# Branch a's gates by seven half-size products a pair, token differences made by transfers in DRAM, and part of a convolution on ScalarE

## The chip, the core and the metric

The kernel runs on one core of a Trainium2 chip. The metric is the device time of one execution in microseconds (us). The core has five engines, each with its own queue of instructions in program order: TensorE (PE; matmuls, with the weight loads shown apart as PEld), VectorE (DVE), ScalarE (ACT), GpSimd (POOL) and SyncE (SP, which issues most transfers). Transfers issued by SP, ACT and POOL run on 16 DMA engines.

## The reference

Two layers of an encoder trunk on 512 tokens of width 1024. Cut to what the change touches:

```python
h = rmsnorm(x, norm_mix[i])
qa, ka, va, glu_in, qc, kc, vc, gates = split(h @ w_in[i])
ya = diff_attention(qa, ka, va, ...)          # 512 wide
yb = conformer_conv(glu_in, ...)              # depthwise, 31 taps, 512 channels, + layernorm
yc = neighbourhood_attention(qc, kc, vc, ...) # 512 wide
ga, gb, gc = split(sigmoid(gates))            # 1024 wide each
merged = ga * (ya @ w_br_a[i]) + gb * (yb @ w_br_b[i]) + gc * (yc @ w_br_c[i])
x = x + merged @ w_o[i]
# then a SwiGLU FFN and a gated per-layer embedding
```

## The kernel before

Everything is kept transposed: 128 channels on the partitions, 512 tokens along the row. A product with a 1024 x 128 block of weights is a loop over 8 chunks of 128 input channels. To keep float32 accuracy in the PE's rounded format (fp32r), every operand is a sum of a high and a low half, and each chunk takes three matmuls (`mm3`, L176 to L181: high x high, high x low, low x high). The halves come from `split` (L162): ACT copies the source into the high half (L143) and DVE subtracts it for the low half (L157).

`weights` (L168) loads a block by SP into `wr` and splits it into `wh` and `wl`, three buffers of each tag. It runs at a raised priority, so that the scheduler places it early. `gemm` (L183) makes a block's products and calls `chunk()` after each chunk. Every four chunks are a tick, on which delayed work (attention units, norms) is emitted into PE's order. PE's order is the order of emission; the other engines' rows are ordered by a list scheduler at build time, by priority and by its own estimate of when inputs are ready, and then run strictly in that order.

A layer (`layer`, L434) runs: GLU inputs; neighbourhood attention (`natten`, branch c); differential attention (`diff`, branch a); gates c (`gate_c`, L751, eight blocks); gates b 0 and 1; branch c (`branch_c`, L758: eight products, each multiplied into `acc[m]`); gates b 2 and 3; `merge_a` (L765); gates b 4 to 7, with parts of the per-layer input between them; `merge_b` (L783); the output product; the FFN; the per-layer embedding.

`merge_a` takes, for each of eight output blocks, a gate product (8 chunks, 24 matmuls of 512 columns), a sigmoid on ACT, a branch product (4 chunks, 12 matmuls), a multiplication and an addition into `acc[m]` on DVE.

The depthwise convolution is DVE's background work. `taps` (L541) is a generator of 4 x 31 operations, each a multiply-add over 128x512 (L160, `conv_z`). `background(after, n)` (L556) emits the next n of them behind a given instruction; the table `BG` says how many at which place. Whatever is left is emitted at the head of `conv` (L568), which sums the four blocks (`conv_ss`), splits the sum (`conv_rp`), and has PE form the mean over channels two ticks later (L581), then the variance and the result for `merge_b`.

The FFN already uses products of half the size. For a pair of blocks (gate g, up u) and a pair of chunks, `seven` (L964) makes both 2 x 2 products of half-size quarters with seven products instead of eight: sums of weights s1 to s4 and differences of activations t1 to t4. Two of the sums are made by accumulating transfers (`accum_op`, L979), which POOL issues. `sevens_of` (L1096) interleaves the pieces of one pair with those of the next.

Each row's right factor `rb` (the rms factor) comes at the start of a layer; `scaled` (L244) multiplies the eight chunks of x by it and makes the high and low halves `h`.

Of the kernel before, what the change touches and what calls it, by code (L numbers as in the profile page):

```python
# [30 lines left out]
CON3W = 31  # L31
HALO = CON3W // 2
NA_KR = 8
NA_KC = 16
# [19 lines left out]
GAP = 144  # L54
BACC = dict(dynamic_dma_scratch_size=1024)
# [6 lines left out]
class Net:  # L62
# [181 lines left out]
    def scaled(self, xs):  # L244

        for k, x in enumerate(xs):
            yield 1
            self.tt(x, x, self.rb, ALU.mult)
            self.hs.append(self.operand(x, self.par(self.i, "mix", k), "h"))

    def main_norm(self, sq, waits=(2, 2), x=None):
# [46 lines left out]
    def build(self):  # L298
        nc, tc, a = self.nc, self.tc, self.a
        self.bufs = dict(wr=3, wh=3, wl=3, h=8, qk=2, kh=2, v=4, pt=2, y=5, z=5, x=4, t=7, rp=4,  # L300
                         e=4, a=3, r=2, rb=1, ss=1, sm=8, rc=4, b=2, s=8)
        self.bg, self.w_ahead = BG, 400
        self.pbufs = dict(mm=3, sc=2, tr=2, av=1)
        with tc.tile_pool(name="sb", bufs=1) as self.pool, \
                tc.tile_pool(name="ps", bufs=1, space=PSUM) as self.psum, \
                tc.tile_pool(name="dr", bufs=1, space=DRAM) as dram:
            xs = dram.tile([KD, P, 512], F32, name="xs")
            self.pis = dram.tile([KD, P, 512], F32, name="pis")
            with tc.manual_schedule(engines={mybir.EngineType.PE}):
# [74 lines left out]
    def small(self):  # L384
# [5 lines left out]
        for tag, n in (("b", 2 * NW), ("s", 10), ("sm", 8), ("rc", 4)):  # L390
            self.sb(tag, [P, n])
        for tag, n in (("lam", 2 * L), ("nlam", L), ("subg", L), ("power", 4)):
            self.sb(tag, [P, n], bufs=1)
# [7 lines left out]
    def consts(self):  # L401
# [5 lines left out]
        self.power = self.sb("power", [P, 4], bufs=1)  # L407
        nc.vector.memset(self.power, -0.5)
        self.ones = self.sb("ones", [P, P], bufs=1)
        nc.vector.memset(self.ones, 1.0)  # L410
# [23 lines left out]
    def layer(self, i, h, xsrc, xs):  # L434
        self.i, self.h = i, h
        zs, cs = [], []
        self.todo = self.taps(zs, cs)
        self.glu(zs)
# [22 lines left out]
        for m in range(1, KD):  # L461
            self.gate_c(acc, m)
        for m in range(2):
            self.gate_b(gb, m, AF.Copy, None)
# [3 lines left out]
        for m in range(2, 4):  # L468
            self.gate_b(gb, m, AF.Sigmoid, "sigmoid")
        self.merge_a(ya, acc)  # L470
        conv = self.run(self.conv(cs, yb))
# [69 lines left out]
    def taps(self, zs, cs):  # L541

        for j, z in enumerate(zs):
            zf = z.rearrange("p a b -> p (a b)")
            c = self.sb("z", [P, 512])
            cs.append(c)
            for d in range(CON3W):
                w = self.par(self.i, "cw", j * CON3W + d)
                src = zf[:, d * GR:d * GR + 512]
                if d == 0:  # L550
                    yield self.nc.vector.tensor_scalar(c, src, w, self.par(self.i, "cb", j),
                                                       ALU.mult, ALU.add)
                else:
                    yield self.stt(c, src, w, c, ALU.mult, ALU.add)

    def background(self, after, n):  # L556
# [194 lines left out]
    def gate_c(self, acc, m):  # L751
        self.phase = "gatec"
        ps = self.proj(OFF_G + 2 * D + m * P)
        if m % 2 == 0:
            acc += self.parts_of("x", [512], 2)
        self.background(self.act(acc[m], ps, AF.Copy), self.bg["gatec"])

    def branch_c(self, acc, ys):  # L758
        self.phase = "branchc"
        for m in range(KD):  # L760
# [4 lines left out]
    def merge_a(self, ys, acc):  # L765
        self.phase = "mergea"
        for m in range(KD):
            ps = self.proj(OFF_G + m * P)
            g = self.sb("t", [P, 512])
            self.background(self.act(g, ps, AF.Sigmoid, table="sigmoid"), self.bg["mergea"])  # L770
            pb = self.ps("mm")
            self.gemm(pb, self.a["w_br_a"][self.i, m], ys)
            self.tt(g, g, pb, ALU.mult)
            self.background(self.tt(acc[m], acc[m], g, ALU.add), self.bg["mergea2"])

    def gate_b(self, gs, m, func, table):
        self.phase = "gateb"
        ps = self.proj(OFF_G + D + m * P)
        if m % 2 == 0:
            gs += self.parts_of("v", [512], 2)  # L780
        self.background(self.act(gs[m], ps, func, table=table), self.bg["gateb"])

# [618 lines left out]
def _halves(w):  # L1401

    b = _blocks(w).reshape(L, NFB, P, KD, P)
    return np.ascontiguousarray(b[:, :, :, ORDER]).reshape(L, NFB, P, D)

# [66 lines left out]
def _layout(v):  # L1472
# [4 lines left out]
    for i in range(L):  # L1477
# [15 lines left out]
        "w_0": w_0,  # L1493
        "w_in": _blocks(w_in),
        "w_va": _vblocks(w_in[:, :, OFF_VA:OFF_VA + 512]),
        "w_vc": _wide(w_in[:, :, OFF_VC:OFF_VC + 512]),
# [25 lines left out]
```

## Time and profile before

| what | value |
|---|---|
| median of 3 runs | 1755.6 us (1755.54 to 1755.67) |
| the profiled execution, its own time | 1756.09 us |
| its span in the profile | 1754.3 us, 25072 instructions |
| granted TensorE clock | 0.999 |
| 38 to 71 us (layer 0, natten's values): DVE busy, ACT busy, DMA share | 32.36, 15.54, 0.60 |
| 71 to 127 us (natten): the same | 39.10, 38.43, 0.67 |
| 279 to 329 us (gates b 0 to 3, branch c): the same | 45.59, 23.71, 0.29 |
| 395 to 423 us (gates b 4 to 7): the same | 22.47, 17.13, 0.41 |

A row of the windows view gives a stretch, its length and each engine's busy time in it. A row of the group view gives source line, engine, operation, output <- inputs with their shapes, the count, and behind the bars the busy time, the mean of one in ns, and the idle time before them with what ended it. The end of a matmul is modelled, so the pace of PE is read from the distance between starts. "Landing" is the time from the issue of a transfer to its completion signal.

### The profile page before, as it was taken

The page shows a single profiled execution, that of the slowest core. Times are in us where ns is not written, and L with a number is a line of the kernel's source. Part 1 is how long each engine was busy: PE and PEld are TensorE (multiplying, and loading weights), DVE is VectorE, ACT ScalarE, POOL GpSimd, SP SyncE. Part 2 cuts the span into 40 slices and gives each one's busy share as a digit, 9 for nine tenths or more (in the row PEclk, how much of TensorE's full clock was granted, in tenths as well). Part 3 has the DMA queues.
Part 4 walks back from the last instruction along what each step waited for, and adds up shares of the span by engine and source line. Part 5 has one row for each costly group of instructions (what it writes and reads, how often), then busy time and mean ns, then how long its engine had stood idle before and what let it go on. Part 6 is the DMA issues. An engine that isn't in the chain of part 4 may idle for free.

```text
span 1754.3 us, 25072 instructions
## 1 busy us (share of the span) xinstructions
PE 1747.3 (100%) x8970; PEld 1490.2 (85%) x8970; DVE 1421.7 (81%) x2346; ACT 964.4 (55%) x1729; POOL 104.0 (6%) x114
## 2 busy tenths in 40 slices
PE   9999999999999999999999999999999999999998
PEld 7888888888888888888888898888888988888887
DVE  7967987998799687797776688889887985977876
ACT  5566545226577275574545665553365763745654
POOL 0000000000121020100000000000001210101000
PEclk9999999999999999999999999999999999999999
DMA  6575641334767365543446655323256764755332
GB/s 230 159 192 158 162 126 46 112 100 140 230 162 186 118 171 155 142 119 131 156 130 164 194 150 153 111 73 96 93 176 199 183 172 121 179 143 157 96 105 97
DMA packets 114781, 253.82 MB, mean 145 GB/s; under 512 B 16864, under 2 KB 23776, under 8 KB 114656
## 3 DMA queue, kind: packets, MB, share of 16 engines
q1 hardware_dynamic: 101264, 227.83, 42.3%
q0 software_dynamic: 12672, 23.07, 8.1%
q8 instruction: 71, 1.16, 0.3%
q10 hardware_dynamic: 720, 1.31, 0.2%
q14 instruction: 54, 0.44, 0.1%
HBM read 215.46 MB, written 7.34 MB: 127 GB/s over the span
## 4 chain that ended last, share of the span: by engine, by line
PE 97%; DVE 1%; DMA 1%; ACT 1%; SPq 0%; issue 0%; POOL 0%; POOLq 0%; ACTq 0%; DVEq 0%
PE ffn_mm L1013 6%; PE ffn_sc L1013 6%; PE ffn_mm L180 4%; PE ffn_mm L179 4%; PE ffn_mm L181 4%; PE ffn_mm L1016 3%; PE ffn_sc L1016 3%; PE mergea_mm L180 2%; PE mergea_mm L181 2%; PE mergea_mm L179 2%; PE ffn_tr L1013 2%; PE natten_mm L179 2%; PE natten_mm L180 2%; PE gateb_mm L180 2%; PE gateb_mm L181 2%; PE gateb_mm L179 2%
## 5 line engine op out<-in xcount | busy, mean ns | idle before, releaser
L160 DVE SCALAR_TENSOR_TENSOR conv_z<-glu_z,pre_par,conv_z 128x512 f32<-128x512 f32 x240 | 179.6, 748 | 3.4
L143 ACT ACTIVATE ffn_wh<-ffn_wr 128x1024 fp32r<-128x1024 f32 (+1 forms) x92 | 92.7, 1021 | 99.5 <-PE ffn_mm L180 63.4
L157 DVE TENSOR_TENSOR ffn_wl<-ffn_wr,ffn_wh 128x1024 fp32r<-128x1024 f32 (+1 forms) x92 | 107.1, 1175 | 20.8 <-ACT ffn_wh L143 20.4
L979 POOL DMA_DIRECT2D ffn_qk<-w_fu x88 | 78.0, 992 | 589.3 <-DMA ffn_qk<-w_fu 323.7
L143 ACT ACTIVATE mergea_wh<-mergea_wr 128x1024 fp32r<-128x1024 f32 (+1 forms) x32 | 27.1, 846 | 96.8 <-PE mergea_mm L180 79.6
L157 DVE TENSOR_TENSOR ffn_t<-ffn_mm,wo_rb 128x512 f32<-128x512 f32 (+1 forms) x46 | 31.1, 677 | 51.6 <-PE ffn_mm L181 51.6
L157 DVE TENSOR_TENSOR ffn_wl<-ffn_qk,ffn_wh 128x1024 fp32r<-128x1024 f32 x44 | 53.7, 1220 | 11.0 <-ACT ffn_wh L143 10.9
L143 ACT ACTIVATE diff_a<-diff_sc,diff_s 128x512 f32<-128x512 f32 x32 | 22.0, 688 | 71.6 <-DVE diff_s L893 71.6
L143 ACT ACTIVATE ffn_wh<-ffn_qk 128x1024 fp32r<-128x1024 f32 x44 | 46.7, 1061 | 26.8 <-PE ffn_mm L180 16.2
L179 PE MATMUL ffn_mm<-ffn_v,ffn_wh 128*128 128x512 f32 x132 | 51.4, 389 | 0.0
L180 PE MATMUL ffn_mm<-ffn_v,ffn_wh 128*128 128x512 f32 x132 | 51.4, 389 | 0.0
L181 PE MATMUL ffn_mm<-ffn_v,ffn_wl 128*128 128x512 f32 x132 | 51.3, 389 | 0.0
L179 PE MATMUL ffn_mm<-ffn_y,ffn_wh 128*128 128x512 f32 x132 | 51.3, 389 | 0.0
L180 PE MATMUL ffn_mm<-ffn_y,ffn_wh 128*128 128x512 f32 x132 | 51.3, 389 | 0.0
L181 PE MATMUL ffn_mm<-ffn_y,ffn_wl 128*128 128x512 f32 x132 | 51.3, 389 | 0.0
L143 ACT ACTIVATE natten_wh<-natten_wr 128x1024 fp32r<-128x1024 f32 x24 | 25.4, 1058 | 42.2 <-issue 15.5
L1013 PE MATMUL ffn_sc<-wo_h,ffn_wh 128*128 128x512 f32 x176 | 48.0, 394 | 0.0
L157 DVE TENSOR_TENSOR ffn_t<-ffn_t,ffn_e 128x256 f32<-128x256 f32 x84 | 46.3, 551 | 1.0 <-ACT ffn_e L143 0.9
L893 DVE TENSOR_REDUCE diff_s<-diff_sc 128x1 f32<-128x512 f32 x64 | 42.1, 683 | 2.2 <-PE diff_sc L800 2.2
L1013 PE MATMUL ffn_mm<-wo_h,ffn_wh 128*128 128x512 f32 x160 | 43.6, 394 | 0.0
L225 POOL TENSOR_TENSOR diff_rc<-diff_sm,pre_power 128x4 f32<-128x4 f32 x8 | 8.9, 1115 | 561.8 <-DVE diff_sm L160 503.2
L143 ACT ACTIVATE natten_b<-natten_b,natten_s 128x256 f32<-128x256 f32 x64 | 30.4, 499 | 20.4 <-DVE natten_s L719 20.3
(894 smaller groups left out, 6050.1 us busy)
## 6 DMA issues: line engine op xcount, KB each, us to landing
ffn_qk<-w_fu POOLq DMA_DIRECT2D x88, 256.0 KB, 6.6
ffn_wr<-w_fg SPq DMA_DIRECT2D x44, 512.0 KB, 4.4
ffn_wr<-w_fd SPq DMA_DIRECT2D x32, 448.0 KB, 3.8
ffn_r<-w_fu SPq DMA_DIRECT2D x44, 256.0 KB, 3.1
ffn_qk<-w_fg SPq DMA_DIRECT2D x44, 256.0 KB, 3.3
ffn_qk<-w_fu SPq DMA_DIRECT2D x44, 256.0 KB, 3.4
natten_wr<-w_in SPq DMA_DIRECT2D x16, 512.0 KB, 4.2
diff_wr<-w_in SPq DMA_DIRECT2D x16, 512.0 KB, 4.3
```

The lines of the kernel that those rows point to most:

```text
L143: i = self.nc.scalar.activation(out, in_, func, **kw)
L157: return self.nc.vector.tensor_tensor(out, a, b, op)
L160: return self.nc.vector.scalar_tensor_tensor(out, a, s, b, op0, op1)
L179: mm(out, wh, ah, start=first, stop=False, **kw)
L180: mm(out, wh, al, start=False, stop=False, **kw)
L181: mm(out, wl, ah, start=False, stop=last, **kw)
L225: nc.gpsimd.tensor_tensor(col, ms, self.power, ALU.pow)
L893: nc.vector.tensor_reduce(out=m[:, u:u + 1], in_=sc, op=ALU.max, axis=AX.X, negate=True)
L979: nc.gpsimd.dma_start(q, wu[:, lo], accum_op=ALU.add)
L1013: mm(out, wh[:, c], bs[k][b], start=first and k == 0, stop=False, skip_group_check=True)
L1016: mm(out[:, 0], wl[:, c], bs[k][b][:, 0], start=False, stop=k == 3, skip_group_check=True)
```

## The change

It has three parts.

**Gates of branch a.** `merge_a` now works on four pairs of gate blocks. `gates` makes the two blocks (call them g and u) of a pair by seven products, each of 4 chunks x 3 matmuls of 256 columns, on quarters of the tokens and channels: a11, s1, s3, a12, s2, a22 and s4 are the names of the weights in this text. a11 and a12 lie in g, a22 in u. s1|s2 is the raw tile: SP loads parts of g and u, and two accumulating transfers on POOL (L869 of the changed kernel) add the other part of u. ACT and DVE split it; then DVE overwrites the same tile with the values of s3 and s4, which are split too. There is one raw tile for all pairs. The three accumulators C, A and Q lie in PSUM; ACT copies C into A after a11, A into Q after s3, and A to SBUF after s2, before s4 adds into A. Between a pair's pieces run the two branch products of the pair before (a "fill": 12 matmuls of 512 columns each); beside the first pair they are the last two of branch c, which `branch_c` no longer does. The addition into `acc` is an accumulating transfer on POOL (L943). The gate weights have a rearranged copy `w_ga`.

**Differences of the activations.** `scaled` lets ACT write signed quarter copies of the normalized x to DRAM, where eight transfers on POOL (four plain, four accumulating, L265) form t1 to t4. `differences` loads them beside branch c, and ACT and DVE split them.

**Convolution.** Of the fourth block's 31 taps the first 16 go to ACT (`aside`): number 0 straight into a tile `half`, numbers 1 to 15 each into the one buffer `rb` (`conv_rb`), from where an accumulating transfer on POOL (L593) adds it into `half`. Ten are placed behind gates c, gates b and pairs (`beside`); the last six are emitted at once, when DVE's taps reach the fourth block, and have no such tie. DVE's remaining 15 taps of that block start from `half`. The counts in `BG` are changed so that they sum to the 108 taps left to DVE.

```diff
-BG = dict(glu=2, natten=1, values=3, diff=1, gatec=2, branchc=2, gateb=4, mergea=4, mergea2=2)
+BG = dict(glu=2, natten=2, values=3, diff=1, gatec=2, branchc=1, gateb=4, mergea=2, mergea2=1, mergea3=2)
...
     def scaled(self, xs):
...
+            f, n = self.sb("t", [P, 2, 256]), self.i * KD + k
+            for half in range(2):
+                g = self.par(self.i, "mix", k) if half == k % 2 else self.neg[:, n:n + 1]
+                self.act(f[:, half], x[:, half * 256:half * 256 + 256], AF.Copy, scale=g)
+            self.nc.gpsimd.dma_start(self.fd[:, k % 2 * 2:k % 2 * 2 + 2, k // 2], f)
...
+        for out, src, add in ((t1, b11, 0), (t3, b22, 0), (t1, b12, 1), (t3, b12, 1), (t2, t1, 0),
+                              (t2, b22, 1), (t4, t2, 0), (t4, b21, 1)):
+            yield 4
+            kw = dict(accum_op=ALU.add) if add else {}
+            self.nc.gpsimd.dma_start(out, src, **kw)
...
+                if j == 3 and d == ASIDE:
+                    for _ in self.other:
+                        pass
+                    yield self.stt(c, src, w, self.half, ALU.mult, ALU.add)
...
+    def aside(self, zs):
+        zf = zs[3].rearrange("p a b -> p (a b)")
+        c, t = self.half, self.sb("rb", [P, 512])
+        for d in range(ASIDE):
...
+            if d == 0:
+                yield self.act(c, src, AF.Identity, scale=w, bias=self.par(self.i, "cb", 3))
+            else:
+                i = self.act(t, src, AF.Copy, scale=w)
+                self.nc.gpsimd.dma_start(c, t, accum_op=ALU.add)
+                yield i
...
+    def gates(self, m, out):
...
+            nc.sync.dma_start(raw[:, lo], wg[:, lo])
+            nc.sync.dma_start(raw[:, up], wu[:, up])
+            nc.sync.dma_start(g, wg)
+            nc.sync.dma_start(a22, wu[:, up])
+            for q in (lo, up):
+                nc.gpsimd.dma_start(raw[:, q], wu[:, lo], accum_op=ALU.add)
+            halve(*wide(), g, ("a11", "a12"))
+            halve(self.sb("kh", [P, 512], F32R), self.sb("a", [P, 512], F32R), a22, ("a22",))
+            halve(*wide(), raw, ("s1", "s2"))
+            self.stt(raw[:, lo], raw[:, lo], -1.0, a22, ALU.mult, ALU.subtract)
+            self.tt(raw[:, up], g[:, up], raw[:, lo], ALU.subtract)
+            for name, q, tag in (("s3", lo, "rp"), ("s4", up, "b")):
+                halve(*(self.sb(tag, [P, 512], F32R) for _ in range(2)), raw[:, q], (name,))
+        C, A, Q = (self.ps("mm", (P, 256)) for _ in range(3))
...
+        product(C, "a11", "b11", True)
+        self.act(A, C, AF.Copy)
+        yield
+        T = self.ps("tr", (P, 256))
+        product(T, "s1", "t3", True)
+        self.act(uu[:, 0], T, AF.Copy)
+        product(A, "s3", "t2")
+        self.background(self.act(Q, A, AF.Copy), self.bg["mergea"])
+        product(C, "a12", "b21")
+        self.act(gg[:, 0], C, AF.Sigmoid, table="sigmoid")
+        yield
+        product(A, "s2", "t1")
+        self.act(uu[:, 1], A, AF.Copy)
+        product(Q, "a22", "t4")
+        self.tt(uu[:, 1], uu[:, 1], uu[:, 0], ALU.add)
+        last = self.tt(uu[:, 0], Q, uu[:, 0], ALU.add)
+        product(A, "s4", "b22")
...
+        def gated(a, pb, m):
+            g = gs[m]
+            self.background(self.tt(g, g, pb, ALU.mult), self.bg["mergea3"])
+            self.nc.gpsimd.dma_start(a, g, accum_op=ALU.add)
...
+            for g in (pair, fill, fill, pair, fill, pair):
+                next(g, None)
```

How the rows stand on the engines. ScalarE before, two blocks in the middle of merge_a (`mergea_wh` is a high half of gate or branch weights, `mergea_t` the sigmoid of a gate):

```order
L143 ACTIVATE mergea_wh_3633<-mergea_wr_3632 128x1024
L143 ACTIVATE mergea_wh_3670<-mergea_wr_3669 128x512
L143 ACTIVATE mergea_t_3602<-mergea_mm_3571 128x512
L143 ACTIVATE mergea_wh_3693<-mergea_wr_3692 128x1024
L143 ACTIVATE mergea_wh_3730<-mergea_wr_3729 128x512
L143 ACTIVATE mergea_t_3662<-mergea_mm_3631 128x512
```

ScalarE in the change, pair 2 (the third) from its copy of A into Q on. `mergea_mm_3830` and `_3831` are its C and A, `gatec_v_3026` is the raw tile, `mergea_wh_4002` the high half of the next pair's s1|s2, `mergea_wh_4035` that of the next fill's weights, `mergea_rp` that of s3, and `mergea_t_3834<-mergea_mm_3831` is the copy of A to SBUF after s2:

```order
L144 ACTIVATE mergea_mm_3832<-mergea_mm_3831 128x256
L144 ACTIVATE mergea_wh_3994<-mergea_wr_3986 128x1024
L144 ACTIVATE conv_rb_2806<-glu_z_920,pre_par_69 128x512
L144 ACTIVATE mergea_t_3833<-mergea_mm_3830 128x256
L144 ACTIVATE mergea_wh_4002<-gatec_v_3026 128x1024
L144 ACTIVATE mergea_wh_4035<-mergea_wr_4034 128x1024
L144 ACTIVATE conv_rb_2806<-glu_z_920,pre_par_69 128x512
L144 ACTIVATE mergea_rp_4008<-gatec_v_3026 128x512
L144 ACTIVATE mergea_t_3834<-mergea_mm_3831 128x256
```

Where a sigmoid stood right behind the splits, two taps (`conv_rb`) and three splits now stand ahead of the copy of A; each tap writes the buffer that the transfer of the tap before it reads.

GpSimd had no row between the last norm of branch a and the norm of the convolution (`conv_rc`). In the change, from the first pair's accumulates (`gatec_v`) to the fourth's:

```order
L593 DMA conv_z_374<-conv_rb_2806 128x512
L869 DMA gatec_v_3026<-w_ga 128x512 x2
L943 DMA gatec_x_1975<-mergea_t_3487 128x512
L943 DMA gatec_x_1975<-mergea_t_3488 128x512
L869 DMA gatec_v_3026<-w_ga 128x512
L593 DMA conv_z_374<-conv_rb_2806 128x512
L869 DMA gatec_v_3026<-w_ga 128x512
L943 DMA gatec_x_2652<-mergea_t_3658 128x512
```

Taps (L593), accumulates for the raw tile (L869) and additions into `acc` (L943) share one queue, and a row waits there until its inputs are ready.

VectorE at the end of merge_a, before (`conv_z` taps, `conv_ss` the sum over blocks, `conv_rp` its low half):

```order
L160 SCALAR_TENSOR_TENSOR conv_z_3544<-glu_z_871,pre_par_67,conv_z_3544 128x512 x3
L157 TENSOR_TENSOR pin_wl_3941<-pin_wr_3939,pin_wh_3940 128x256
L160 SCALAR_TENSOR_TENSOR conv_z_3544<-glu_z_871,pre_par_67,conv_z_3544 128x512
L157 TENSOR_TENSOR conv_ss_3867<-conv_ss_3867,conv_z_3544 128x512
L157 TENSOR_TENSOR mergea_t_3842<-mergea_t_3842,mergea_mm_3846 128x512
L157 TENSOR_TENSOR pin_wl_3957<-pin_wr_3955,pin_wh_3956 128x256
L157 TENSOR_TENSOR gatec_x_2884<-gatec_x_2884,mergea_t_3842 128x512
L157 TENSOR_TENSOR conv_rp_3872<-conv_ss_3867,conv_rp_3871 128x512
```

And in the change, from the last pair's quarter add after the copy of A (`mergea_t_4020`), `conv_z_374` being `half`:

```order
L158 TENSOR_TENSOR mergea_t_4020<-mergea_t_4020 128x256
L161 SCALAR_TENSOR_TENSOR conv_z_3900<-glu_z_920,pre_par_69,conv_z_374 128x512
L158 TENSOR_TENSOR mergea_t_4020<-mergea_mm_4018,mergea_t_4020 128x256
L161 SCALAR_TENSOR_TENSOR conv_z_3900<-glu_z_920,pre_par_69,conv_z_3900 128x512
L158 TENSOR_TENSOR pin_e_4211<-pin_t_4208,pin_e_4210 128x512
L161 SCALAR_TENSOR_TENSOR conv_z_3900<-glu_z_920,pre_par_69,conv_z_3900 128x512
L158 TENSOR_TENSOR pin_e_4217<-pin_t_4214,pin_e_4216 128x512
L161 SCALAR_TENSOR_TENSOR conv_z_3900<-glu_z_920,pre_par_69,conv_z_3900 128x512
L158 TENSOR_TENSOR mergea_t_4019<-mergea_t_4019,mergea_sc_4166 128x512
L161 SCALAR_TENSOR_TENSOR conv_z_3900<-glu_z_920,pre_par_69,conv_z_3900 128x512 x3
```

All 15 taps of the fourth block now stand behind the last pair's copy of A, where one of the last few stood before.

More of the change, by code (lines that the diff above doesn't have):

```diff
@@ L462, in layer @@
             self.gate_c(acc, m)
+        self.bs, self.raw = [], self.sb("v", [P, 1024])
         for m in range(2):
@@ L763, in branch_c @@
             self.background(self.tt(acc[m], acc[m], ps, ALU.mult), self.bg["branchc"])
-    def merge_a(self, ys, acc):
-        self.phase = "mergea"
[L767 to L774, printed above, removed]
+            next(quarters, None)
```

134 lines of the change are left out of this document (122 added, 12 removed).

## The prediction

> **What bounds the kernel now.** I read the busy shares first, then the chain that ended last, then PE's waits, then the stretch that the change rewrites.
>
> ```profile
> PE 1747.3 (100%) x8970; PEld 1490.2 (85%) x8970; DVE 1421.7 (81%) x2346; ACT 964.4 (55%) x1729; POOL 104.0 (6%) x114
> PE 97%; DVE 1%; DMA 1%; ACT 1%; SPq 0%; issue 0%; POOL 0%; POOLq 0%; ACTq 0%; DVEq 0%
> ...
> PE pre_av L331 <- DVE pre_zeror L404: 1.1, 1, 1.1
> PE diff_sc L800 <- ACT diff_e L143: 0.2, 1, 0.2
> ...
> 329.00:362.00 33.00, 33.00 (x147) 27.35 (x146) 29.44 (x41) 9.56 (x14) 0.00 (x0) 1.00 0.27 85
> 362.00:395.00 33.00, 33.00 (x148) 27.31 (x147) 29.85 (x41) 8.87 (x14) 0.00 (x0) 1.00 0.33 103
> ```
>
> PE is the chain (97%) and waits 1.3 us in all: a matmul less is time less, and any new wait of PE is time more, at full price. The window rows are merge_a of layer 0 (stretch, length, then busy PE, weight loads, DVE, ACT, POOL, granted clock 1.00, DMA share 0.27 and 0.33). DVE is busy 59.3 of 66 us there, ACT only 18.4. So ACT has room in sum; whether it has it at the right moment is the question.
>
> **What PE saves.** First and last row of a run of 512-wide and of a run of 256-wide matmuls:
>
> ```profile
> 345.30 0.39 PE L179 MATMUL mergea_mm<-glu_h,mergea_wh 128*128 128x512 f32 x1
> ...
> 350.74 0.39 PE L179 MATMUL mergea_mm<-diff_y,mergea_wh 128*128 128x512 f32 x1
> ...
> 495.62 0.28 PE L1020 MATMUL ffn_tr<-wo_v,ffn_wh 128*128 128x256 f32 x1
> ...
> 498.36 0.28 PE L1022 MATMUL ffn_mm<-wo_z,ffn_pt 128*128 128x256 f32 x1
> ```
>
> 24 matmuls of 512 in 5.44 us are 227 ns each; 23 of 256 in 2.74 us are 119 ns. Two gate blocks cost 48 x 0.227 = 10.88 us, seven products 84 x 0.119 = 10.00 us. Saved: 0.88 us a pair, 7.0 us over eight pairs. Nothing else on PE changes. By the Trainium skill ("TensorE: Matmul & The Clock Gate", Back-to-back issue gap) an isolated matmul takes N/2.4 + 2.5 ns, so about 216 and 109 ns, an estimate of 1.2 us a pair and 9.5 us in all; the rows say 227 and 119 with the clock at 1.00, so the sum keeps 7.0.
>
> **Prices of the operations.** These rows price what ACT, DVE and the transfers do in the new merge_a:
>
> ```profile
> L143 ACT ACTIVATE mergea_wh<-mergea_wr 128x1024 fp32r<-128x1024 f32 x7 | 7.4, 1062 | 13.9 <-PE mergea_mm L180 9.6 <-PE gateb_mm L180 4.3
> L143 ACT ACTIVATE mergea_wh<-mergea_wr 128x512 fp32r<-128x512 f32 x7 | 4.4, 633 | 30.2 <-PE mergea_mm L180 30.2
> L143 ACT ACTIVATE gateb_v<-gateb_mm 128x512 f32<-128x512 f32 x4 | 2.3, 579 | 0.0
> L143 ACT ACTIVATE ffn_t<-ffn_mm 128x256 f32<-128x256 f32 x82 | 30.3, 372 | 12.0 <-PE ffn_mm L1016 12.0
> ...
> L160 DVE SCALAR_TENSOR_TENSOR conv_z<-glu_z,pre_par,conv_z 128x512 f32<-128x512 f32 x47 | 35.2, 749 | 0.8
> L157 DVE TENSOR_TENSOR mergea_wl<-mergea_wr,mergea_wh 128x1024 fp32r<-128x1024 f32 x7 | 8.6, 1226 | 1.2 <-ACT mergea_wh L143 0.6
> L157 DVE TENSOR_TENSOR mergea_t<-mergea_t,mergea_mm 128x512 f32<-128x512 f32 x8 | 5.5, 688 | 2.0 <-PE mergea_mm L181 2.0
> L157 DVE TENSOR_TENSOR pin_wl<-pin_wr,pin_wh 128x256 fp32r<-128x256 f32 x1 | 0.4, 426 | 0.1
> ...
> DMA to landing us min/median/max: 4.0/6.6/9.8
> ...
> DMA to landing us min/median/max: 4.4/4.7/5.1
> ...
> L979 POOL DMA_DIRECT2D ffn_qk<-w_fu x88: 862/886/1248, 448.0 to 1621.0; - x88
> mergea_wr<-w_br_a SPq DMA_DIRECT2D x16, 256.0 KB, 2.6
> ```
>
> The only accumulating transfers of before are the FFN's 88 (256 KB each, the size of every new one): 0.9 us on POOL, and 4.0 us at least from issue to landing, 6.6 in the median; the two at 489 to 492 us, where few others run, took 4.4 and 5.1. The change's are SBUF to SBUF, which no row shows, in a stretch with a DMA share of about 0.3. Bounds: 2.6 us (a plain 256 KB load in this very stretch) and 6.6. I take 4.0, the nearest row at the lightest load.
>
> In sum DVE fits. Per pair it has 3 wide low halves (3.7 us), 5 operations of 0.69 to 0.75 for a22, s3 and s4 (3.6), two quarter adds (0.9), two products (1.4) and 7 taps (5.2): 14.8 us beside 15.45 us of PE. The 16 quarter copies in `scaled` (16 x 0.37 = 6 us a layer) and the 16 transfers for the differences I cost at nothing: they have from about 45 to 290 us. Without that cover, NATTEN's weights and stacked transfers would wait; I allow 0 to 4 us a layer.
>
> **What PE loses.** ACT, DVE and POOL run their rows in order (ACT's waits on PE in the rows above show it), so an ACT row that waits for a transfer holds the copies behind it. With a pair's start as 0, PE's pieces end at: a11 1.4, fill 4.2, s1 5.6, s3 7.0, a12 8.4, fill 11.2, s2 12.6, a22 14.0, s4 15.4. s4 adds into A, so it needs ACT's copy of A after s2: only a22 (1.4 us) covers it. Four places follow, per layer:
>
> 1. Front of pair 0. After the last gate_b matmul ACT does an eviction 0.6, a tap 0.6, the split of s1|s2 1.0 and only then that of the fill's weights 1.0; DVE follows with two low halves. The third matmul of the fill finds its low half at 4.7 and should run at 1.9: 2.8 us. The accumulate for s1|s2 stands on POOL behind the tap that waits for gate_b 2 and lands 0.4 us after ACT could use it: 3.2 us.
> 2. End of pairs 0 and 1. Ahead of the copy of A on ACT stand the next pair's s1|s2 split, which itself waits for s2 (its buffer), and the split of the next fill's weights. The copy ends at 12.7 + 1.0 + 1.0 + 0.4 = 15.1 and was due at 14.0: 1.1 us. In pair 0 the raw tile comes free late (low half of s4 at 9.0; plain loads 3.1, then 0.9 + 0.1 on POOL and 4.0 to land: 17.1; copy done 19.5 against 17.2): 2.3 us there.
> 3. End of pairs 2 and 3. The last six taps (10 to 15) share one buffer, so each ACT row waits for the transfer before it: 0.6 + 0.1 + 4.0 us a turn. In pair 2, as worked below, the copy of A ends at 17.8: 3.8 us. In pair 3 the same turns put taps 12 to 15 at 2.4, 7.1, 11.9 and 16.6; then three splits (gate_b's weights, two for pin) and the copy of A at 18.8: 4.8 us.
>
> ```
> POOL  accumulate for pair 3 at 6.5, tap 9 at 7.4, landed 11.4
> ACT   tap 10 11.5-12.1, sigmoid 12.5, s1|s2 of pair 3 (after s2) 12.8-13.8, fill weights 14.7
> ACT   tap 11 (tap 10 landed 12.2+4.0) 16.3-16.9, s3 split 17.4, copy of A 17.8
> ```
>
> 4. The convolution's mean. DVE's 15 taps of the fourth block start from `half`, so after tap 15 has landed, at 20.7 from pair 3's start; PE ends s4 at 20.2. From there DVE does 15 taps (11.2), four operations of 0.69, one of 1.23, two of 0.43 and the last sum (0.69): 16.8, about 15.8 with the overlap of 0.08 that the rows below show between starts and ends. conv_ss is done 0.5 + 15.8 = 16.3 after s4, the split's high half at 17.1. PE wants it after two fills (5.4) and a gate block (5.4), at 10.9: 6.2 us.
>
> ```profile
> 372.65 0.69 DVE L157 TENSOR_TENSOR gatec_x<-gatec_x,mergea_t 128x512 f32<-128x512 f32 x1
> 373.26 2.32 DVE L160 SCALAR_TENSOR_TENSOR conv_z<-glu_z,pre_par,conv_z 128x512 f32<-128x512 f32 x3
> ...
> 396.07 0.69 DVE L157 TENSOR_TENSOR conv_rp<-conv_ss,conv_rp 128x512 fp32r<-128x512 f32 x1
> ...
> 399.70 0.39 PE L581 MATMUL conv_tr<-conv_rp,pre_onesr 128*128 128x512 f32 x1
> ```
>
> Before, the low half was there at 396.8 and PE used it at 399.7: 2.9 us in hand, now gone.
>
> Sum per layer: 3.2 + 2.3 + 1.1 + 3.8 + 4.8 + 6.2 = 21.4; both layers 42.8. The profiled execution took 1756.1 (its span is 1754.3, 1.8 lie around it), 0.5 above the median of 1755.6. So 1756.1 - 7.0 + 42.8 = 1791.9, and 1791 from the median.
>
> **Rivals.**
>
> *The saving alone* (faster): 1755.6 - 7.0 = 1748.6. For it: the FFN runs the same seven products, accumulates and copies with PE at 100% (chain). Against: there, another pair's products lie between s2 and s4, and no tap stands among ACT's copies. 0.10. Some stalls that just eat the saving (within 0.2%): 0.04.
>
> *Only the order costs* (slower): transfers land in 2.6 us, as the plain load does. Then no tap holds ACT: 2.8 + 1.0 + 1.1 + 2.3 (pair 2: the two wide splits, a tap, and s3's split wait for DVE) + 0.9 + 5.2 = 13.3 a layer, 1755.6 - 7.0 + 26.6 = 1775. The Trainium skill ("DMA: Bandwidth & Descriptors", Anatomy of one DMA — SWDGE (gpsimd) path) has 2.0 us fixed plus bytes over 436 GB/s, an estimate of 2.6 us for 256 KB, with most of the fixed part in the receipt, heaviest for HBM. The rows above, all of them into SBUF, never fall below 4.0, so the trace differs so far. 0.27.
>
> *Long transfers* (slower): 6.6 us, the median. Each turn of a tap grows by 2.6: by the same steps 10.9, 2.9, 8.9, 15.1 and 8.7, 46.5 a layer, 1842. It decides where merge_a's transfers collide as the FFN's do; its DMA share of 0.3 speaks against. 0.10.
>
> *A change that does not do what it says*: the order shows all of it done; not weighed further.
>
> **How the numbers follow.** Forecast 0.49 at 1791, order alone 0.27, long 0.10, saving alone 0.10, cancelled 0.04. A measurement of this kernel tells 0.2% (3.5 us) from no change. Faster 0.10, same 0.04, slower 0.86. The range runs from 1766, under the order's 1775 (its small terms may halve), to 1826, part of the way to the long transfers (and the 4 us a layer of early transfers): about 0.2 is left out.
>
> **What would show it.** PE waits on ACT before the s4 products, growing from pair 0 to pair 3, some 4 us in the last two; ACT's `conv_rb` rows waiting on the accumulating transfer; conv's first matmul waiting about 6 us on DVE or ACT; mean pace of 256-wide matmuls 119 ns. The forecast is wrong if those waits are absent, if taps land in under 3 us, or if PE waits in NATTEN.

## The result and the profile after

The changed kernel takes 1828.5 us (median of 4 runs, 1827.6 to 1829.7) against 1755.6 before: ratio 1.0415, 95% interval 1.0397 to 1.0433. It is slower, by 72.9 us; the prediction had +35 and a range that ended at 1826. The profiled execution spans 1827.0 us, so 1828.8 with the 1.8 around it, 72.7 more than the 1756.1 that the prediction started from.

From the page of the changed kernel, busy time by engine and a row of the 40 slices (granted clock in tenths); then PE's waits (engine, line, what it waited for: us in total, times, longest):

```profile
PE 1769.6 (97%) x9258; PEld 1518.3 (83%) x9258; DVE 1427.7 (78%) x2366; ACT 1030.3 (56%) x1867; POOL 182.4 (10%) x208
PEclk9999999898999999999999999998899999999999
```
```profile
PE mergea_mm L180 <- ACT mergea_t L144: 26.5, 8, 5.4
PE branchc_sc L180 <- ACT branchc_wh L144: 8.8, 2, 4.5
PE conv_tr L629 <- ACT conv_rp L144: 8.8, 2, 4.4
PE natten_mm L732 <- DVE natten_t L161: 4.1, 1, 4.1
PE diff_tr L230 <- POOL diff_rc L226: 1.9, 2, 1.4
PE pre_av L349 <- DVE pre_zeror L422: 1.1, 1, 1.1
PE branchc_sc L182 <- DVE branchc_wl L158: 0.6, 2, 0.4
```

Where there was 1.3 us of waiting, there are now 51.8. The first three rows and the last are the places that the prediction named: the s4 products, the first fill, the mean of the convolution, 44.7 us in both layers (42.8 predicted). NATTEN's 4.1 was costed at nothing. And the PE busy time **grew** by 22 us although PE has 7 us less to do: it ran slow. These windows of the changed kernel (stretch, length, busy PE, granted clock, DMA share, GB/s) follow pairs 0 and 1 of layer 0:

```profile
331.00:337.00 6.00, 1.93 (x15) 1.00 0.75 125
337.00:341.00 4.00, 3.38 (x8) 0.57 0.31 90
341.00:352.00 11.00, 11.00 (x78) 1.00 0.70 181
352.00:356.00 4.00, 0.67 (x4) 0.81 0.03 5
356.00:362.00 6.00, 6.00 (x29) 0.56 0.70 235
362.00:374.00 12.00, 11.91 (x81) 1.00 0.70 132
374.00:376.00 2.00, 1.31 (x11) 1.00 0.50 89
376.00:390.00 14.00, 14.00 (x98) 1.00 0.80 198
```

Behind the waits of 4.3 and 3.3 us the granted clock is half for some 3 to 6 us; behind the wait of 0.8 at 374 it is not. Added up over windows of 1 us (busy PE times one minus the clock), 25.6 us go to it in the whole run, 2.9 of them in NATTEN. The Trainium skill ("TensorE: Matmul & The Clock Gate", Part 1: The HAM clock gate) has this rule: after an idle window of about 3.4 us PE drops to half rate until it has been busy for about as long, the window running free. The trace agrees in kind, with a wait of 2.28 us at 1258.4 in layer 1 that was also followed by it.

This table has the time from the first matmul of one stage to the first of the next, read from the rows of PE in the timeline (us); "f2" is the last experiment:

| stretch | before | after | f2 |
|---|---|---|---|
| NATTEN, layer 0 (layer 1) | 88.6 (88.4) | 95.5 (88.4) | 89.7 (88.5) |
| gate_b to merge_a, layers 0, 1 | 49.8, 49.8 | 45.1, 46.0 | 45.9, 46.8 |
| merge_a to the mean | 70.7, 70.7 | 105.8, 103.5 | 73.8, 73.6 |
| mean to merge_b | 23.2, 23.2 | 26.3, 26.4 | 23.2, 23.2 |
| FFN | 336.2, 336.3 | 336.2, 336.3 | 336.6, 336.6 |

In merge_a two columns of branch_c moved in from the stretch ahead (5.4 us). By the prediction's figures PE needs 4 x (10.0 + 5.44) + 10.9 = 72.7 us there. The loss is in that stretch, in the slow clock just behind it, and in NATTEN of layer 0. FFN, nearly two fifths of the kernel and with the same kind of gates, did not change.

What made merge_a slow shows in the rows around the raw tile `gatec_v` in pair 0 (start, duration, engine; in brackets the idle time before and its releaser):

```profile
335.20 1.06 ACT L144 ACTIVATE mergea_wh<-gatec_v 128x1024 fp32r<-128x1024 f32 x1 [2.46 <-DMA gatec_v<-w_ga]
...
342.90 0.68 DVE L158 TENSOR_TENSOR mergea_b<-gatec_v,mergea_b 128x512 fp32r<-128x512 f32 x1
343.61 0.33 SPq L865 DMA_DIRECT2D gatec_v<-w_ga  x1
346.60 0.88 POOL L869 DMA_DIRECT2D gatec_v<-w_ga  x1 [12.57 <-DMA gatec_v<-w_ga]
353.19 1.06 ACT L144 ACTIVATE mergea_wh<-gatec_v 128x1024 fp32r<-128x1024 f32 x1 [3.81 <-DMA gatec_v<-w_ga]
354.15 1.04 ACT L144 ACTIVATE mergea_wh<-mergea_wr 128x1024 fp32r<-128x1024 f32 x1
355.10 0.36 ACT L144 ACTIVATE mergea_t<-mergea_mm 128x256 f32<-128x256 f32 x1
355.52 0.58 PE L180 MATMUL mergea_mm<-glu_h,mergea_b 128*128 128x256 f32 x1 [3.33 <-ACT mergea_t L144]
```

The first row is pair 0's own s1|s2 split, held by its accumulates. Then one loop: the low half of s4 frees the tile, a plain load refills it (3.0 us), POOL adds to it (6.6 us from there to ACT's row), the next s1|s2 is split, the next fill's weights are split, A is copied, and only then s4 runs. POOL had been idle for 12.6 us by then, the last 3.0 of them for this load. Each raw tile takes two accumulates, one for each half. The landing times of the taps (L593) and of the raw tile's accumulates (L869):

```profile
L593 POOL DMA_DIRECT2D conv_z<-conv_rb x30: 855/872/1145, 273.4 to 1317.1; - x30
...
DMA to landing us min/median/max: 3.2/3.2/7.0
```
```profile
L869 POOL DMA_DIRECT2D gatec_v<-w_ga x16: 870/1170/1531, 328.4 to 1286.1; - x16
...
DMA to landing us min/median/max: 4.0/5.4/6.3
```

The taps (from SBUF) land in 3.2 us in the median, the raw tile's accumulates (from DRAM) in 5.4, where the prediction had 4.0 for both. The first of each two landed in 4.0 to 5.6 us, the second, issued 0.5 to 1.8 us behind it, in 5.3 to 6.3, and the split waits for both. The two kinds also get into each other's way on POOL:

```profile
380.86 0.70 ACT L144 ACTIVATE conv_rb<-glu_z,pre_par 128x512 f32<-128x512 f32 x1
382.94 0.87 POOL L869 DMA_DIRECT2D gatec_v<-w_ga  x1 [9.90 <-DMA gatec_v<-w_ga]
383.57 1.13 POOL L593 DMA_DIRECT2D conv_z<-conv_rb  x1
```

ACT was done with this tap at 381.56, but POOL first waited for the plain load of the raw tile. Other taps reach POOL 0.4 us after ACT's row; this one came 2.0 us after it, and it landed in 5.6 us instead of 3.2. The same tap of layer 1 came 1.3 us after ACT's row and landed in 5.3.

### The profile page after: what moved, and what is told of

The parts are those of the page before. It is cut to its first block, busy times and chain, and to the rows that moved or that the text cites. A ratio compares the mean times of both kernels' runs of the same rounds, so it can differ in the third digit from the quotient of the medians.

```text
span 1827.0 us, 26061 instructions
## 1 busy us (share of the span) xinstructions
PE 1769.6 (97%) x9258; PEld 1518.3 (83%) x9258; DVE 1427.7 (78%) x2366; ACT 1030.3 (56%) x1867; POOL 182.4 (10%) x208
## 5 line engine op out<-in xcount | busy, mean ns | idle before, releaser
L161 DVE SCALAR_TENSOR_TENSOR conv_z<-glu_z,pre_par,conv_z 128x512 f32<-128x512 f32 x210 | 157.0, 747 | 4.5 <-DMA conv_z<-conv_rb 1.6
L158 DVE TENSOR_TENSOR ffn_wl<-ffn_qk,ffn_wh 128x1024 fp32r<-128x1024 f32 x44 | 53.6, 1218 | 11.0 <-ACT ffn_wh L144 10.9
L593 POOL DMA_DIRECT2D conv_z<-conv_rb x30 | 27.0, 899 | 180.5 <-ACT conv_rb L144 128.7
```

The source lines that it names most:

```text
L158: return self.nc.vector.tensor_tensor(out, a, b, op)
L161: return self.nc.vector.scalar_tensor_tensor(out, a, s, b, op0, op1)
L593: self.nc.gpsimd.dma_start(c, t, accum_op=ALU.add)
```

## The experiments

Every run was timed beside the kernel before (1755.9 to 1756.4 us). By mere count, the slow clock's 25.6 us and 7.7 us more of waiting than predicted (51.8 - 1.3 - 42.8) nearly fill the missing 37 us. But a count doesn't say what would come back if one of them went. Two theories were at hand: the slow clock as a price of its own on every wait, or a chain of ACT, DVE and transfers that was longer than worked out, with PE's slow stretches inside the time that it would have waited anyway.

### Is the clock a price of its own?

Idle matmuls (results unread) ahead of the waiting products keep PE at work:

```diff
+    def keep(self, n):
+        t = self.ps("av", (P, 256))
+        a = self.h[0][:, 0, 0:256]
+        for _ in range(n):
+            self.nc.tensor.matmul(t, self.h[0][:, 0, 0:P], a, start=True, stop=True)
...
+        self.keep({0: 18, 2: 0, 4: 30, 6: 40}[m])
         product(A, "s4", "b22")
```

> The changed kernel with idle matmuls (128x256, results unread) put on PE ahead of the places where it waits in merge_a: 34 before the first fill, 18, 0, 30 and 40 before the s4 products of pairs 0 to 3, 34 before the mean of the convolution. No wait is taken away; PE is only kept at work in it. Theory A (each wait of over 2 us also halves PE's clock for some us behind it, 25.6 us in all, about 3 of them in NATTEN where nothing is put): the granted clock goes from 0.983 to about 0.997 and the time from 1828.5 to about 1806 (1800 to 1815), though 312 matmuls are added. Rival B (PE runs slow there for another reason, the transfers or the engines beside it): clock and time stay, 1828 or more.

Measured 1829.9 (1.0416, 1.0401 to 1.0432): the time did not change, as rival B had it, although the slow clock's 25.6 us were cut to 12.3. The idle matmuls had run past the operands' arrival in places, so they were refitted:

> The filled kernel with the idle matmuls cut to the waits that they met there: 32 before the first fill, 18, 0 and 26 before the s4 products of pairs 0 to 2, 30 before pair 3's s3 product (where PE then waited 4.5 us) and none before its s4, 20 before the mean. In the first try the idle matmuls ran some 10.7 us past the moment at which the operands were there (4.5 and 3.1 us of it in layer 0 before pair 3's s4 and the mean). Theory A (the half clock behind a wait lengthens the path, 22 us in merge_a): about 1808. Rival B (merge_a and the mean are bound by the transfers and by ScalarE's rows, and PE's slow stretches lie in time that it would wait in any case): about 1826. The first try less its overrun, 1819, lies between: then the clock is about half of the missing time.

Measured 1835.3 (1.0450): neither number, and longer than both. In pair 3 and in layer 1 the refitted matmuls again missed the waits, so the sum of this run says little. Its first two pairs are clean, and they do say something. Windows of that run:

```profile
331.00:337.00 6.00, 5.39 (x45) 1.00 0.73 122
337.00:341.00 4.00, 3.27 (x14) 1.00 0.37 112
341.00:352.00 11.00, 11.00 (x84) 1.00 0.70 174
352.00:356.00 4.00, 2.49 (x21) 1.00 0.02 4
356.00:362.00 6.00, 6.00 (x42) 1.00 0.63 196
362.00:373.00 11.00, 8.40 (x60) 1.00 0.87 180
```

The clock is 1.00 throughout, where the changed kernel lost 1.5 + 2.9 = 4.4 us to it. Yet s4 of pair 1 starts 42.2 us after merge_a's first matmul, against 43.4: of 4.4 us, 1.1 came back, and pair 1's wait grew from 0.8 to 2.8. So in these two pairs PE is not what the others wait for: the slow clock there is mostly time that it would have waited. Where PE alone sets the pace, the clock is a price: from the mean to merge_b the changed kernel takes 26.3 us, the first filled run 23.2, as before.

### ScalarE's taps

Eight of them earlier, tied to the copies of q and k:

```diff
-            self.act(raw, ps, AF.Copy, scale=1.0 if s else 0.125)
+            self.beside(self.act(raw, ps, AF.Copy, scale=1.0 if s else 0.125))
```

> The changed kernel with eight of ScalarE's taps tied to the copies of the differential branch's q and k, so that all 16 are through before merge_a. Theory A (ACT is held by the last taps' transfers, which share one buffer): the waits before s4 of pairs 2 and 3 (4.7 and 5.4 us) fall to the order's 2.3 and 0.9, the convolution's mean (4.4) falls below 2, and the slow clock behind them goes too: 1828.5 - 2 x (2.4 + 4.5 + 3) - about 12 of clock = about 1797 (1785 to 1805). Rival B (the splits that stand ahead of the copy of A do it alone): pairs 2 and 3 stay as they are, only the mean gets earlier: about 1815.

Measured 1801.4 (1.0260, 1.0245 to 1.0275), near theory A: pair 3 and the mean wait no more, pair 2 still 2.6 and 1.8; merge_a to the mean fell to 88.7 and 90.0 us. In return the stages from the differential branch to gate_b take 5 us a layer longer.

All of them back on VectorE (`ASIDE = 0`):

> The changed kernel with ScalarE's 16 taps back on VectorE, the seven-product gates and the transferred differences kept. Theory A: the waits of pairs 2 and 3 fall to the order's 1 to 2.3 us, but VectorE gets 16 x 0.66 = 10.6 us more in a stretch where it is full, so the convolution's mean waits some 10 us or more: 1815 to 1840. Rival B (the taps' transfers are the whole cost of the change): about 1755.

Measured 1816.2 (1.0336, 1.0318 to 1.0353), as theory A had it: the mean waits 12.2 us in each layer. VectorE can't take the taps back with these gates; but the transferred taps as placed cost 12 us more than even that.

Two buffers for the taps:

```diff
-        c, t = self.half, self.sb("rb", [P, 512])
+        c = self.half
...
+                t = self.sb("rb", [P, 512])
...
-e=4, a=3, r=2, rb=1, ss=1, sm=8, rc=4, b=2, s=8)
+e=4, a=3, r=2, rb=2, ss=1, sm=8, rc=4, b=2, s=7)
```

> The changed kernel with two buffers for ScalarE's taps in place of one. Theory A (terms 3 and 4 of the prediction: ScalarE is held by the transfer of the tap before): the waits before s4 of pairs 2 and 3 (4.7 and 5.4 us) fall to the order's 2.3 and 0.9, the mean still waits for the chain of transfers: 1828.5 - 2 x (2.4 + 3) - some clock = about 1815. Rival B (the order and the raw tile hold ScalarE): within 3 us of 1828.

Measured 1824.7 (1.0389): 3.8 us, nearer to rival B. Pair 3's s4 waits no more (a fill there does, by 2), but pair 2 keeps 5.2 and 4.1, and the mean 6.1 and 4.6. (With `s=7` the FFN takes 0.8 us a layer longer; that is in the sum.) The taps' buffer alone is not what holds ACT.

### The order on ScalarE

The copy of A ahead of the next splits:

```diff
-        self.act(uu[:, 1], A, AF.Copy)
+        with self.tc.high_priority(offset=min(900, self.tc.cur_priority - self.p0)):
+            self.act(uu[:, 1], A, AF.Copy)
```

> The changed kernel with ACT's copy of A (which s4 needs) ahead of the next fill's weight split, and in pairs 1 and 2 ahead of the tap beside it. Theory A (ACT's row order behind s2 makes the wait): the waits before s4 of pairs 0 to 2 (3.3, 0.8, 4.7 in layer 0; 2.3, 1.1, 3.7 in layer 1) fall below 1 us each, pair 3 stays at about 5, and with the slow clock behind them some 20 us go: about 1808 (1800 to 1816). Rival B (s4 waits for its own halves or for the transfers, not for the copy): the waits stay, 1828.

Measured 1825.4 (1.0394): a miss. Pair 0's wait before s4 falls to 0.4 in layer 0, and pair 1's grows to 3.0, the mean's to 6.9 and 9.5. Repaired at one place, the time was lost at the next. The same with all taps early and the first fill ahead:

> All taps early and the first fill ahead, as in the run at 1796.6, with the copy of A ahead of the next splits, but one raw tile. Theory A (the order on ScalarE makes the waits of 1.9 to 3.8 us that are left): 1796.6 - 14 = about 1783, merge_a to the mean 80 us in place of 87. Rival B (the raw tile makes them): the waits move to the s1 products and the time stays within 4 us of 1796.

Measured 1795.3 (1.0220) against 1796.6 without it: rival B. The order on ACT, the price of the prediction's first two terms, is not what binds as long as there is one raw tile.

### The raw tile

A second one, paid for with a small buffer and one for scores:

```diff
-        self.bs, self.raw = [], self.sb("v", [P, 1024])
+        self.bs, self.raws = [], [self.sb("v", [P, 1024]) for _ in range(2)]
...
-        nc, raw = self.nc, self.raw
+        nc, raw = self.nc, self.raws[m // 2 % 2]
...
-v=4, pt=2, y=5, z=5, x=4, t=7, rp=4,
+v=5, pt=2, y=5, z=5, x=4, t=6, rp=4,
-b=2, s=8)
+b=2, s=7)
```

> The changed kernel with a second raw tile for s1|s2 and nothing else (it takes one of the seven small buffers, which costs FFN 0.8 us a layer, as the run before showed). Theory A (the single raw tile makes the loop that paces merge_a: low half of s4, plain loads 3 us, accumulates 5.4 us, split): from merge_a's first matmul to the mean 105.8 us become about 96, time about 1810. Rival B (the taps' transfers pace pairs 2 and 3 and the mean, and PE only waits there for longer): pairs 0 and 1 gain 3 us, the rest gives it back, 1825 or more.

Measured 1812.1 (1.0318, 1.0302 to 1.0333), theory A; this run is called y1 below. Merge_a to the mean takes 94.6 and 96.9 us, against 105.8 and 103.5: the single tile cost 11.2 and 6.6 us there. Its PE waits:

```profile
PE branchc_sc L180 <- ACT branchc_wh L144: 10.4, 2, 5.7
PE mergea_mm L180 <- ACT mergea_t L144: 10.0, 4, 3.9
PE conv_tr L629 <- ACT conv_rp L144: 8.6, 2, 4.3
```

The s4 products wait four times instead of eight, 10.0 us instead of 26.5: pairs 0 and 1 not at all, pairs 2 and 3 of layer 0 by 1.2 and 3.9. The taps gained little: ACT still waits 36.0 us in all for their transfers (35.9 in the changed kernel), and the mean still waits 4.3. So it is the raw tile's own loop that went.

### NATTEN of layer 0

The eviction that PE waits for, ahead on VectorE:

```diff
-                self.stt(t, ps, f, self.rb, ALU.mult, ALU.mult)
+                with self.tc.high_priority(offset=min(200, self.tc.cur_priority - self.p0)):
+                    self.stt(t, ps, f, self.rb, ALU.mult, ALU.mult)
```

> The changed kernel with the eviction on VectorE that frees NATTEN's first accumulator put ahead of the low halves of the weights and of h again, as it stood before the change. Theory A: the 4.1 us wait in NATTEN of layer 0 goes, and the 6.6 us at half clock behind it too (3.3 us more): 1828.5 - 7.4 = 1821. Rival B (the clock costs nothing by itself): 1824.4. Rival C (the early transfers make NATTEN wait at the next place): 1828.

Measured 1826.8 (1.0404; single runs from 1823.0 to 1832.2, too wide to tell B from C): the wait fell to 2.3 us only, the stage from 95.5 to 92.6. A row of the changed kernel points to the reason:

```profile
47.59 0.51 ACT L144 ACTIVATE glu_t<-pre_x,pre_neg 128x256 f32<-128x256 f32 x1 [0.96 <-DMA fd<-glu_t]
```

ACT stood waiting for a small buffer that a transfer to DRAM was still reading. So only that buffer was changed:

```diff
-            f, n = self.sb("t", [P, 2, 256]), self.i * KD + k
+            f, n = self.sb("rp", [P, 2, 256]), self.i * KD + k
```

> The changed kernel with the quarter copies of the normed input written to buffers that lie idle then, in place of the seven shared small ones. Theory A (the early transfers to DRAM hold those buffers, ScalarE waits for one, and NATTEN's eviction comes late): the 4.1 us wait in NATTEN of layer 0 and its slow clock (together 6.9 us from glu's end to the differential stage) go: 1828.5 - 7 = 1821.5. Rival B (ScalarE's and VectorE's work for the 16 copies itself makes NATTEN late): 1826 or more.

Measured 1822.0 (run z3; 1.0372, 1.0358 to 1.0386): theory A. The wait is 0.2 us, the stage 89.7. It is 1.1 us longer than in the kernel before; 0.5 of them are two short waits, and where the rest goes is not shown.

### All of it together

All taps by gate_c, and the first fill's weights split ahead of s1|s2:

```diff
-        if m > 3:
+        if m > 0:
             self.beside(last)
...
-            for g in (pair, fill, fill, pair, fill, pair):
+            for g in (fill, pair, fill, pair, fill, pair) if n == 0 else (pair, fill, fill, pair, fill, pair):
```

> All 16 taps of ScalarE tied to the copies of q, k and gate_c, none beside gate_b or in merge_a, and the first fill's weights split ahead of s1|s2. Theory A: against the run with eight early taps (1801) the wait at the first fill (4.8 and 5.0 us) and its slow clock (2 us each) go: about 1787. Rival B (the wait moves to s1, whose accumulated tile lands later than the split is wanted): 1795 to 1800.

Measured 1796.6 (run x8; 1.0226), rival B: the first fill's wait went, and up to 1.9 us came back at s1, s3 and the next fill. With the second raw tile, the copy of A ahead and the NATTEN eviction:

> As the run before, with a second raw tile for s1|s2, the copy of A ahead of the next splits, and the NATTEN eviction put back; one buffer fewer for small temporaries. Theory A (the order on ScalarE and the single raw tile make the rest of the waits in merge_a): no wait over 1 us is left in merge_a, about 1787 - 7 - 16 = 1764. Rival B (VectorE is full in merge_a and the waits move to its rows): 1775 or more.

Measured 1778.9 (run x9; 1.0129): by its time rival B (1775 or more), but not for B's reason. Merge_a to the mean takes 78.8 us, against 87.1 in the run before, and no wait over 1 us is left in it but the one for the first s1 (2.3). The time went elsewhere: the stages from the differential branch to gate_b take 157.7 and 157.8 us, 151.4 in the changed kernel. With the first two pairs' tiles summed before gate_b, and the taps spread over more of the program:

```diff
+            if head:
+                self.beside(i)
...
+        for m in (0, 2):
+            self.summed(m)
         for m in range(2):
             self.gate_b(gb, m, AF.Copy, None)
```

(`i` is the copy of q or k, and `summed` holds the plain loads and accumulates of `gates`.)

> The run with two raw tiles (1778.9), with the first two pairs' raw tiles summed before gate_b's weights are called for, the taps spread from the second differential head to gate_b's second block, and NATTEN's eviction given more priority. Theory A: the waits left (5 us a layer at the front of merge_a, 5 to 6 us a layer in the differential stage, 2.5 in NATTEN) go: about 1757 (1752 to 1765), level with the kernel before. Rival B (VectorE and ScalarE are too full beside the taps for it): 1768 or more.

Measured 1769.6 (run y4; 1.0079), in rival B's range (1768 or more): merge_a to the mean 73.5 and 73.6, the clock 0.999, but the stages from the differential branch to gate_b, where most of the taps now stand, take 4 to 5 us a layer longer. Then the taps in branch_c instead, with the idle buffers of z3, in two variants:

```diff
-            self.background(self.tt(acc[m], acc[m], ps, ALU.mult), self.bg["branchc"])
+            last = self.tt(acc[m], acc[m], ps, ALU.mult)
+            self.background(last, self.bg["branchc"])
+            self.beside(last)
```

> Two raw tiles, the first two pairs summed early, the fill ahead, the copy of A ahead, quarter copies in idle buffers, and ScalarE's taps beside gate_c from block 2 on, gate_b and the columns of branch_c. Theory A: no wait over 1 us is left before FFN but POOL's power in branch_c (1 to 2 us), FFN pays 0.8 us a layer for the buffer: 1756 - 7 + 1.6 + 3 + 2 = about 1755 (1750 to 1760). Rival B (ScalarE's taps hold its copies in branch_c, where a transfer takes 4 us and a column 5.4): 1765 or more.

> As the run before, but the second raw tile is paid for with one of three probability buffers of the differential stage in place of a small one. Theory A: FFN gets its 1.6 us back: about 1753. Rival B (the differential stage or FFN needs the third buffer): 1760 or more.

Measured 1779.9 and 1785.5 (runs z1 and z2), both misses, in rival B's range. PE waited for a norm's power on POOL, in z1 6.0 us in each layer. In layer 0 DVE had the sum for it at 314.4, but a tap stood ahead of it on POOL until 317.6, so about 3.2 of the 6.0 us are the tap's: ACT could write it only when the transfer of the tap before it had landed. And FFN's 0.8 us stayed though z2 left the small buffers (`t`) at seven: it had come in every kernel with `s=7`, the buffers for scores. Both changed back (shown against the changed kernel):

```diff
+            if head > 1 and s:
+                self.beside(i)
...
-        if m > 3:
-            self.beside(last)
+        self.beside(last)
...
-sm=8, rc=4, b=2, s=8)
+sm=7, rc=4, b=2, s=8)
```

> Two raw tiles with the first two pairs summed early, the fill and the copy of A ahead, quarter copies in idle buffers; ScalarE's taps: two beside the last two differential heads, eight beside gate_c, four beside gate_b, two in pairs 0 and 1 of merge_a, none in branch_c; the buffer paid for by a small one of the norms, not by the scores. Theory A: waits of PE below 8 us in all, NATTEN 1 us, the differential stage 1 to 2 us a layer, merge_a to the mean 73.5 to 75: 1756 - 7 + 8 = about 1757 (1751 to 1761), level with the kernel before. Rival B (the change costs more than that wherever the taps stand): 1765 or more.

Measured 1759.5 (run f2; 1.0022, 1.0012 to 1.0031), theory A. Its PE waits are down to these, and the clock is 1.00:

```profile
PE diff_tr L230 <- POOL diff_rc L226: 3.6, 2, 2.3
PE pre_av L349 <- DVE pre_zeror L422: 1.1, 1, 1.1
PE diff_tr L230 <- DVE diff_pt L158: 1.0, 2, 0.5
PE diff_tr L216 <- ACT diff_ss L144: 0.8, 1, 0.8
PE natten_av L795 <- DVE natten_pt L158: 0.3, 1, 0.3
PE natten_mm L734 <- DVE natten_t L161: 0.2, 1, 0.2
PE mergea_mm L182 <- DVE mergea_rp L158: 0.2, 1, 0.2
```

So 69 of the 73 us were a matter of buffers and places, not of the idea. But no version here beats the kernel before: this one is slower by 3.6 us, and the interval leaves out 1. NATTEN takes 1.1 us more, the stages from the differential branch to gate_b 0.1 and 2.4, the FFN 0.7 in both layers together; from gate_b to the mean only 1.0 comes back.

## Why the prediction went wrong

**The sign and the places were right.** PE waited where it was said: in front of pair 0, before the s4 products, before the mean. ACT's `conv_rb` rows waited for the taps' transfers (35.9 us, 18 times), and the 256-wide matmuls kept their pace of 0.12 us. In layer 1 the four s4 waits are within 0.3 us of the forecast; in layer 0 they miss it by up to 1.0. The front came out 1.5 us longer and the mean 1.8 shorter (us; measured in layer 0, layer 1):

| place | predicted | measured |
|---|---|---|
| front of pair 0 | 3.2 | 4.7, 4.7 |
| s4 of pairs 0, 1 | 2.3, 1.1 | 3.3, 0.8; 2.3, 1.1 |
| s4 of pairs 2, 3 | 3.8, 4.8 | 4.7, 5.4; 3.7, 5.1 |
| mean | 6.2 | 4.4, 4.4 |
| sum | 21.4 | 23.4, 21.3 |

**The step that failed: the size of terms 1 and 2**, the raw tile's part. That the sums agree is luck. Counted from merge_a's first matmul in layer 0 (331.33), this is when s4 of pairs 0 to 3 and the mean start:

| | pair 0 | pair 1 | pair 2 | pair 3 | mean |
|---|---|---|---|---|---|
| predicted (pieces plus waits) | 19.5 | 36.0 | 55.3 | 75.5 | 94.1 |
| after | 24.2 | 43.4 | 63.9 | 86.6 | 105.8 |
| second raw tile (y1) | 22.3 | 37.9 | 54.9 | 76.1 | 94.6 |

The operands came 4.7 us later than worked out in pair 0, and 11.7 by the mean. PE came later too, because it ran at half clock behind each wait, so that each wait by itself looked like the forecast. Without that loop, with the second raw tile, the mean starts at 94.6 (96.9 in layer 1, where the changed kernel has 103.5). That the last three moments lie within 0.6 us of the predicted ones in layer 0 is again partly luck: the forecast holds 3.4 us of waits in pairs 0 and 1 that this run does not have, and the run has a front 1.5 us longer and slow stretches; in layer 1 they are 0.4, 1.7 and 2.8 late. What the single tile cost is the difference, 11.2 and 6.6 us in the two layers, with the slow stretches that went with it. The prediction had charged it 0.4 us a layer at the front and 2.3 in pair 0 (low half of s4 at 9.0, landed at 17.1). In layer 0 it was 12.3 and 21.9: the first accumulates kept ACT idle for 2.5 us instead of 0.4, DVE's low half stood behind the product of the first fill, which PE had not finished, and POOL took 6.6 us from its row to ACT's instead of 5.0. For this landing the prediction went by transfers "SBUF to SBUF"; the taps are that, but the raw tile's accumulates read `w_ga` in DRAM, as the FFN's do. The tile also held pair 1, whose s4 starts at 37.9 instead of 43.4 without it, and once a layer a tap on POOL's queue; no term had either.

**The early transfers, "costed at nothing"**, cost 6.9 us in NATTEN of layer 0 (stage 95.5 against 88.6), above the bound of 4. With the copies in other buffers and the same transfers (z3) 5.8 of them went, so it was mainly the shared buffer and not bandwidth. In layer 1 they were free. The prediction said that a wait in NATTEN would prove it wrong, and there it was.

**No term for the clock.** It adds 3.1 us a layer behind the mean's wait and 2.9 in NATTEN, where PE is the bound. In merge_a it is mostly a companion of the waiting (1.1 of 4.4 us came back in the two clean pairs). For layer 1, and for pairs 2 and 3, this was not settled cleanly.

**What adds up**: the merge_a stretch 11.7 + 9.4 over the forecast, behind the mean 3.1 + 3.2, NATTEN 6.9, the first stage 0.7 (it differs by as much between kernels that share it): 35.0 of the 36.9 that were missing.

**The rivals.** "Long transfers" (1842) was the nearest in mechanism and in time: accumulates from DRAM did land in 5.4 us, but those of the taps in 3.2. "Only the order costs" fell, since no tap landed in less than 3.1 us and ACT did wait for them; "saving alone" fell with the result. And the saving is smaller than 7.0: in f2, gate_b to the mean takes 119.7 us with 1.5 of waiting (120.4 with 2.3 in layer 1), 120.5 before, so 2.4 a layer in place of 3.5; why is not shown.

## What to carry to other kernels

A tile that is loaded, added to by a transfer, read and refilled is a loop with a period of its own; add its steps round the whole circle, with the slowest landing of its kind, and count it on every turn, also for what stands behind it on an in-order queue. Short waits that match a forecast prove little when the engine that waits has itself become late: compare the moments, not the gaps. A copy that a transfer has yet to read holds its buffer, so look at who else draws from that pool before costing the transfer at nothing.

## What was not expected of the hardware

Accumulating transfers of 256 KB landed in 3.2 us (median of 30, source and target in SBUF) and in 5.4 (median of 16, source in DRAM); in the last run it was 3.7 and 5.4. Those from DRAM were issued in twos, and the first of two landed in as little as 4.0.

After waits of PE as short as 1.8 us the granted clock was 0.50 (1.76 us at 187.2 in x8, 1.82 at 1279.7 in y1), while waits of 2.4 us in NATTEN of x9 and y4 left it at 1.00. In the changed kernel the slow stretches start at 337.43, 354.49, 395.45 and so on, always a multiple of 3.41 us apart, and last 3.41 or 6.83. So how a wait lies on that grid may decide, and not its length alone; no run tests this.
